# A decayed running sum behind a matrix product: another order of the channels on the partitions

## The chip, the cores and the metric

The kernel runs on one core of a Trainium2 chip. The core has five engines that work side by side, each through its own list of instructions in order: TensorE (PE in the profile; its weight loads are PEld) multiplies matrices, VectorE (DVE), ScalarE (ACT) and GpSimd (POOL) work on elements, SyncE (SP) issues transfers. Transfers (DMAs) move data between the main memory and the on-chip memory SBUF, which has 128 partitions; TensorE writes its products to a second on-chip memory, PSUM. Engines wait for each other and for transfers through semaphores.

The metric is the device time of one execution in microseconds (us). The profile shows one such execution, in which each instruction has a start and a duration.

## The reference

```python
def setup_inputs():
    B, S, D = (16, 2048, 1024)
    return {'x': np.random.randn(B, S, D).astype(np.float32), 'w': np.random.randn(D, D).astype(np.float32), 'decay': (0.9 * np.random.rand(D) + 0.05).astype(np.float32)}

def reference(x, w, decay):
    xw = x @ w
    out = np.zeros_like(xw)
    out[:, 0, :] = xw[:, 0, :].copy()
    for t in range(1, S):
        out[:, t, :] = decay[None, :] * out[:, t - 1, :] + xw[:, t, :]
    return out.astype(np.float32)
```

A product of 32768 rows with a 1024 x 1024 matrix, and then, along each of 16 sequences of 2048 steps, a running sum per output channel in which the sum so far is multiplied by that channel's decay at each step.

## The kernel before, in words

**Tiling.** The rows are cut into 64 chunks of 512 time steps (`TL`), and two chunks form a group, except that the last two are taken one by one. Each group (or single chunk at the end) gives eight output tiles `n` of 128 output channels: 31 x 8 + 2 x 8 = 264 tiles. A tile is the product of eight weight blocks `k` (`K` = 8), accumulated in PSUM, 512 columns per matmul.

**How x gets onto the partitions.** The product needs the 1024 input channels on the partitions. `load` (line 105, issued on GpSimd's queue, four transfers per chunk) brings a chunk into `xb` and converts it to bfloat16 on the way: partition 32q + t' holds, for each of 16 blocks of 32 time steps (`j`), the 256 channels of quadrant q at time step t' of the block. These 256 channels are 128 words of 4 bytes, each a pair of neighbouring channels. `turn` (line 115) then has VectorE transpose blocks of 32 partitions x 32 words into `xw`, so that time runs along the row and each partition holds four words' worth (`M` = 4) of channels. The instruction takes an access pattern for its input: per block j and per m, 32 words `c` that go to the 32 partitions of the quadrant. `part` (line 123, ScalarE mostly) splits the pairs, from `xw` into `xt`, the operand of the matmuls. There are 62 turns of a whole chunk (2048 words per partition) and, for the first two chunks, 16 turns of an eighth each (256 words), so that work can start early.

**How w gets there.** `w` must lie with the same input channels on the same partitions. It comes in four quarters `(h, e)`: h is the half of the output columns (512 of them), e the even or odd channel of the pairs. `load_w` (line 313) loads a quarter into a staging area (`stage`) by four transfers. The first quarter goes over the queues of SyncE and ScalarE (two each), the other three over GpSimd's, between and behind the transfers of the first chunks of x. `settle` (line 320) copies one m of a quarter, 128 partitions x 512 columns, into the weights `wsb` as bfloat16; VectorE and ScalarE share these copies. The opening's order of work is written out in `agenda[-99]`: M are half chunks of x, U the later quarters of w, W and w the settles (VectorE and ScalarE), E the turns of an eighth, F and G the parts.

**From the tile to the output.** A tile's running sum is formed in one of two ways. Unpaired: VectorE scans the PSUM tile directly (`run`, line 233, 1024 elements). Paired: ScalarE copies the tile to `xs` (line 186) and multiplies its even steps by the decay (line 169), GpSimd adds them to the odd steps (`join`, line 208), VectorE scans the 512 sums with the squared decay (line 213), ScalarE multiplies the results by the decay (`even`, line 169) and GpSimd fills in the other steps (`fill`, line 260). Paired operations read or write every second element of a row, a step of 8 bytes. At the end VectorE transposes the tile back (`back`, line 272), and when four tiles of a group are there, SyncE's queue stores them (line 296).

**Order.** All instructions are pinned in program order per engine. `agenda` writes the order out for the first 34 tiles and the last 20; between them `usual` does, per tile, the copy of this tile, the scan and the completion of the last one, the output turn of the one before, and `later` puts the turns (T) and parts (X, Y) of a coming chunk at fixed tiles ahead of their use: two full turns per group of eight tiles. VectorE thus has, in one list, the turns, the scans and the output turns.

Of the kernel before, what the change touches and what calls it, by code (L numbers as in the profile page):

```python
# [14 lines left out]
def _ap(ap_obj: bass.AP, new_ap, extra_offset=0):  # L15
    return dataclasses.replace(
        ap_obj,
        ap=[list(p) for p in new_ap],
        offset=ap_obj.offset + extra_offset,
    )  # L20
# [5 lines left out]
def kernel(  # L26
# [27 lines left out]
    pin = tc.keep_in_program_order  # L54
    B, S, D = x.shape
# [3 lines left out]
    P = 32  # L59
    CQ = D // NQ  # L60
    K = CQ // P
    M = K // 2
# [4 lines left out]
    CH = D // 2  # L67
# [8 lines left out]
    def ring(pool, name, count, shape, dtype=FP32):  # L76
        i = turns[name] = turns.get(name, -1) + 1
        return pool.tile(shape, dtype, name=f"{name}{i % count}")

    def quad(q):  # L80
        return slice(q * P, (q + 1) * P)
# [28 lines left out]
    def turn(c, j0=0, j1=NJ, m0=0, m1=M):  # L110
        if c not in xw_of:
            xw_of[c] = ring(sb, "xw", 2, [128, M, NJ, P, 2], BF16)
        src = xb_of[c][:, j0:j1].rearrange("p j c -> p (j c)").bitcast(FP32)
        dst = xw_of[c].rearrange("p m j i e -> p (m j i e)").bitcast(FP32)
        pin(nc.vector.transpose(  # L115
            out=dst.rearrange("p (m j i) -> p j m i", m=M, i=P)[:, j0:j1, m0:m1],
            in_=src.rearrange("p (j m c) -> p j m c", m=M, c=P)[:, :, m0:m1]))

    def part(c, copy, m0, m1, j0=0, j1=NJ):
        if c not in xt_of:  # L120
# [159 lines left out]
    class Outlet:  # L280
# [8 lines left out]
        def store(self, b, t0):  # L289
# [4 lines left out]
            for j in range(0, self.nj, nj):  # L294
# [11 lines left out]
    stage = {(0, 0): room[0][:, 0:size],  # L306
             (0, 1): room[0][:, size:size * 3 // 2].bitcast(BF16),
             (1, 0): room[1][:, 0:size // 2].bitcast(BF16),
             (1, 1): room[1][:, size // 2:size].bitcast(BF16)}

    def load_w(queues, h, e):
        for i, q in enumerate((0, 2, 1, 3)):
            pin(queues[i % len(queues)].dma_start(  # L313
                out=stage[h, e][quad(q)].rearrange("p (m d) -> p m d", m=M),
                in_=_ap(w, [[2 * D, P], [2 * P * D, M], [1, CH]],
                        (q * CQ + e) * D + h * CH)))

    def settle(h, e, m, copy):
        src = stage[h, e][:, m * CH:(m + 1) * CH]
# [5 lines left out]
    rows = const.tile([128, 2, P], FP32, name="rows")  # L325
    touch = const.tile([128, 1], BF16, name="touch")
    load_w((nc.sync, nc.scalar), 0, 0)
    pin(nc.vector.memset(idle, 0.0))  # L328
    pin(nc.vector.memset(rows, 0.0))
# [13 lines left out]
    for q in range(NQ):  # L343
        pin(nc.sync.dma_start(
            out=rows[q * P:q * P + R],
            in_=_ap(decay, [[P, R], [CH, 2], [1, P]], q * CR)))
# [10 lines left out]
    def load_part(i):  # L357
        load_w((nc.gpsimd,), *((0, 1), (1, 0), (1, 1))[i])
# [76 lines left out]
    def turn_and_load(c):  # L435
        turn(c)
        if 2 <= c < nch - 3:
            loads.extend((c + 3, q) for q in range(NQ))
# [14 lines left out]
        "M": load_half,  # L453
        "U": load_part,
        "E": lambda i: turn(i // 8, *halves[i // 4 % 2], i % 4, i % 4 + 1),
        "F": lambda i: part_one(i, nc.vector.tensor_copy),
        "G": lambda i: part_one(i, nc.scalar.copy),
# [218 lines left out]
```

## Time and profile before

| | |
|---|---|
| time, median of 3 runs | 904.32 us (903.89 to 904.64) |
| profiled execution, time | 904.34 us |
| profiled execution, span of the core | 902.5 us |
| mean granted TensorE clock | 0.999 of full speed |
| busy: TensorE / VectorE / ScalarE / GpSimd | 896.7 / 824.2 / 686.9 / 656.6 us |
| full turns, line 115 | 62 x 2284 ns |
| turns of an eighth, line 115 | 16 x 414 ns |
| issues of w on GpSimd, line 313 | 12 x 544 ns |

The span runs from the first to the last instruction that the profile shows; what is missing to the execution's time, 904.34 - 902.5 = 1.84 us, lies around it. In lines on groups of instructions, the columns are line, engine, operation, output <- input, shapes, count, then busy us, mean ns of one instruction, and after the second bar the idle time of the engine just before them with what ended it. In a timeline each line has start, duration, engine, line and operation, with the idle time before it in brackets. In lines on waits, the numbers are us in total, how many times, and the longest.

### The profile page before, as it was taken

Reading aid. Unit: us, or ns where it says so; the run is one execution under the profiler, and the core shown is the slowest. Engines: PE = TensorE matmul, PEld = TensorE weight load, DVE = VectorE, ACT = ScalarE, POOL = GpSimd, SP = SyncE. Lnnn points to the kernel's source line nnn. Section 1 sums busy time; section 2 is a strip of 40 time slices with the busy share of each in tenths; the row PEclk is TensorE's granted clock in tenths of the full one; section 3 lists DMA queues with packets and bytes.
Section 4 is the critical chain, followed back from the end, with each engine's and each line's share of the span. In section 5 each row is a group of like instructions: output and inputs, shape, how many; then the busy total and the mean of one; then the engine's idle time right before and its main releaser. Section 6 shows DMA issues by size and latency. Waiting matters only on the chain.

```text
span 902.5 us, 12285 instructions
## 1 busy us (share of the span) xinstructions
PE 896.7 (99%) x4201; PEld 411.4 (46%) x4201; DVE 824.2 (91%) x632; ACT 686.9 (76%) x958; POOL 656.6 (73%) x755
## 2 busy tenths in 40 slices
PE   9999999999999999999999999999999999999998
PEld 5544444444444444444444444444444444444444
DVE  4999998998999999999998999999999999999998
ACT  4889867777877877878778778777787787787743
POOL 7888678777767768777677687777777776876632
PEclk9999999999999999999999999999999999999999
DMA  9999999999999999999999999999999999999858
GB/s 193 194 215 220 231 231 206 215 231 243 251 249 248 242 251 246 244 250 253 227 236 228 221 228 230 232 227 227 232 230 228 227 234 223 228 226 218 183 142 236
DMA packets 403182, 204.77 MB, mean 227 GB/s; under 512 B 9392, under 2 KB 402096, under 8 KB 403120
## 3 DMA queue, kind: packets, MB, share of 16 engines
q1 hardware_dynamic: 265808, 134.77, 60.8%
q0 software_dynamic: 137024, 68.70, 56.8%
q8 instruction: 33, 0.54, 0.2%
q10 hardware_dynamic: 288, 0.52, 0.2%
q14 instruction: 29, 0.24, 0.1%
HBM read 138.42 MB, written 134.22 MB: 302 GB/s over the span
## 4 chain that ended last, share of the span: by engine, by line
PE 98%; DMA 1%; POOL 0%; issue 0%; DVE 0%; DVEq 0%; POOLq 0%
PE ps L131 96%; PE spare L131 1%; DMA xb<-in_x_dram 1%; DMA ot<-in_w_dram 1%; POOL ot L313 0%; PE spare L398 0%; PE ps L398 0%; DVE h L416 0%; DVE wsb L320 0%; DVEq L320 0%; POOLq L660 0%
## 5 line engine op out<-in xcount | busy, mean ns | idle before, releaser
L131 PE MATMUL ps<-xt,wsb 128*128 128x512 bf16 x4016 | 866.1, 378 | 0.5 <-DVE wsb L320 0.5
L131 PEld LDWEIGHTS <-wsb 128*128 128x128 bf16 x4152 | 405.9, 98 | 479.7 <-ACT wsb L320 0.8
L208 POOL TENSOR_TENSOR xs<-h,xs 128x512 f32<-128x512 f32 (+1 forms) x190 | 242.5, 1276 | 187.1 <-ACT h L169 85.5
L186 ACT COPY xs<-ps 128x1024 f32<-128x1024 f32 (+1 forms) x190 | 188.9, 994 | 152.8 <-PE ps L131 147.7
L272 DVE STREAM_TRANSPOSE ot<-so 128x1024 f32<-128x1024 f32 (+2 forms) x264 | 300.1, 1175 | 4.5 <-DMA out_dram<-ot 2.3
L260 POOL TENSOR_TENSOR so<-h,xs 128x512 f32<-128x512 f32 (+1 forms) x190 | 241.1, 1271 | 45.2 <-ACT h L169 28.0
L123 ACT COPY xt<-xw 128x2048 bf16<-128x2048 bf16 (+1 forms) x136 | 242.2, 1789 | 7.8 <-DVE xw L115 7.8
L105 POOL DMA_DIRECT2D xb<-in_x_dram x264 | 174.0, 660 | 3.5 <-DMA ot<-in_w_dram 1.1
L169 ACT ACTIVATE h<-so,dec 128x512 f32<-128x512 f32 (+1 forms) x190 | 145.4, 766 | 29.8 <-DVE so L213 26.7
L115 DVE STREAM_TRANSPOSE xw<-xb 128x2048 f32<-128x2048 f32 (+1 forms) x78 | 147.3, 1900 | 7.0 <-DMA xb<-in_x_dram 7.0
L213 DVE TENSOR_TENSOR_SCAN so<-spare,keep,xs 128x512 f32<-128x512 f32 (+1 forms) x97 | 119.8, 1237 | 25.7 <-POOL xs L208 25.4
L213 DVE TENSOR_TENSOR_SCAN so<-spare,xs 128x512 f32<-128x512 f32 x93 | 113.1, 1218 | 26.5 <-POOL xs L208 23.6
L169 ACT ACTIVATE h<-ps,dec 128x512 f32<-128x512 f32 (+1 forms) x189 | 129.4, 685 | 0.0
L233 DVE TENSOR_TENSOR_SCAN so<-dec,ps 128x1024 f32<-128x1024 f32 x34 | 76.7, 2259 | 1.0 <-ACT h L169 1.0
L233 DVE TENSOR_TENSOR_SCAN so<-dec,keep,ps 128x1024 f32<-128x1024 f32 (+2 forms) x35 | 75.4, 2153 | 0.0
L264 ACT COPY keep<-so 128x1 f32<-128x1 f32 x136 | 25.2, 188 | 9.4 <-DVE so L233 9.0
L204 ACT COPY so<-keep 128x1 f32<-128x1 f32 x97 | 18.5, 192 | 2.7 <-DVE ot L272 2.5
L131 PE MATMUL spare<-xt,wsb 128*128 128x512 bf16 (+1 forms) x56 | 11.9, 341 | 0.0
L131 PE MATMUL ps<-xw,wsb 128*128 128x256 bf16 (+1 forms) x68 | 11.2, 301 | 0.0
L202 POOL MEMSET so<- 128x1 f32 x93 | 10.6, 116 | 0.6 <-DVE ot L272 0.6
L313 POOL DMA_DIRECT2D ot<-in_w_dram x12 | 6.5, 544 | 3.2 <-DMA xb<-in_x_dram 2.1
L338 PE MATMUL spare<-idle 128*128 128x512 bf16 x22 | 7.5, 519 | 1.2 <-DVE idle L328 1.2
(39 smaller groups left out, 39.3 us busy)
## 6 DMA issues: line engine op xcount, KB each, us to landing
out_dram<-ot SPq DMA_DIRECT2D x236, 512.0 KB, 10.9
xb<-in_x_dram POOLq DMA_DIRECT2D x248, 256.0 KB, 7.9
out_dram<-ot SPq DMA_DIRECT2D x56, 128.0 KB, 2.6
xb<-in_x_dram POOLq DMA_DIRECT2D x16, 128.0 KB, 5.8
out_dram<-ot SPq DMA_DIRECT2D x8, 256.0 KB, 4.2
ot<-in_w_dram POOLq DMA_DIRECT2D x12, 128.0 KB, 5.1
out_dram<-xb SPq DMA_DIRECT2D x3, 256.0 KB
ot<-in_w_dram ACTq DMA_DIRECT2D x2, 256.0 KB, 5.1
```

The lines of the kernel that those rows point to most:

```text
L105: pin(nc.gpsimd.dma_start(out=xb_of[c][quad(q), j0:j1], in_=_ap(x, [[D, P], [P * D, j1 - j0], [1, CQ]], (b * S + t0 + j0 * P) * D + q * CQ)))
L115: pin(nc.vector.transpose(out=dst.rearrange("p (m j i) -> p j m i", m=M, i=P)[:, j0:j1, m0:m1], in_=src.rearrange("p (j m c) -> p j m c", ...
L123: pin(copy(out=xt_of[c][:, m0:m1, :, j0 * P:j1 * P], in_=src))
L131: pin(nc.tensor.matmul(out=ps[:, t0:t1] if ps.shape[1] >= t1 else ps, lhsT=lhs, rhs=rhs, start=(k == 0 and t0 == start), stop=(k == K - 1),))
L169: pin(nc.scalar.activation(out=h, in_=src, func=mybir.ActivationFunctionType.Copy, scale=dec[:, self.n:self.n + 1]))
L186: pin(nc.scalar.copy(out=self.xs[:, i * size:(i + 1) * size], in_=ps))
L208: pin(nc.gpsimd.tensor_tensor(out=odds, in0=self.g, in1=odds, op=ALU.add))
L213: pin(nc.vector.tensor_tensor_scan(out=so[:, 3:T + 2:2], data0=squares[-1][:, n:n + 1].to_broadcast([128, T // 2]), data1=self.xs[:, 1:T:2 ...
L233: pin(nc.vector.tensor_tensor_scan(out=so[:, t + 2:t + 2 + size], data0=dec[:, n:n + 1].to_broadcast([128, size]), data1=ps, initial=befor ...
L260: pin(nc.gpsimd.tensor_tensor(out=self.so[:, 2:T + 2:2], in0=self.h, in1=self.xs[:, 0:T:2], op=ALU.add))
L264: pin(nc.scalar.copy(out=self.keep, in_=self.so[:, self.T + 1:self.T + 2]))
L272: pin(nc.vector.transpose(out=outlet.ot[:, :, c0:c0 + P], in_=self.so[:, 2 + t0:2 + t0 + nj * P].rearrange("p (i t) -> p i t", t=P)))
```

## The change

Two access patterns change. In `before`, word 32m + c of a quadrant's 128 words goes to partition c of the quadrant, in block m: partition 32q + c holds channels 256q + 64m + 2c + e. In the changed kernel it is word 4c + m: partition p = 32q + c holds channels 8p + 2m + e, so that the 1024 channels lie at one stride of eight channels over all 128 partitions. The transposing instruction writes as before, and reads words that lie four words (16 bytes) apart within each run of 32, where it read neighbouring words.

The rows of w follow the same order. A quarter's four transfers were one per quadrant, each into 32 partitions with four rows of 512 columns per partition, from rows that lie two rows apart. Now there is one per m, each into all 128 partitions with one row of 512 columns per partition, from rows that lie eight rows apart. Bytes, transfers and their queues stay; a settle reads what one transfer brings, where it read parts of all four. Every engine issues the same instructions in the same order. Below line 317, line numbers are one lower in the changed kernel.

```diff
@@ turn
         pin(nc.vector.transpose(
             out=dst.rearrange("p (m j i) -> p j m i", m=M, i=P)[:, j0:j1, m0:m1],
-            in_=src.rearrange("p (j m c) -> p j m c", m=M, c=P)[:, :, m0:m1]))
+            in_=src.rearrange("p (j c m) -> p j m c", m=M, c=P)[:, :, m0:m1]))
@@ load_w
     def load_w(queues, h, e):
-        for i, q in enumerate((0, 2, 1, 3)):
-            pin(queues[i % len(queues)].dma_start(
-                out=stage[h, e][quad(q)].rearrange("p (m d) -> p m d", m=M),
-                in_=_ap(w, [[2 * D, P], [2 * P * D, M], [1, CH]],
-                        (q * CQ + e) * D + h * CH)))
+        for m in range(M):
+            pin(queues[m % len(queues)].dma_start(
+                out=stage[h, e][:, m * CH:(m + 1) * CH],
+                in_=_ap(w, [[K * D, 128], [1, CH]], (2 * m + e) * D + h * CH)))
```

## The prediction

> **What bounds the kernel now.** I read the totals first, then the chain that ended last, then the windows by stage, then VectorE's groups, waits and timeline. The totals and the chain, from the page:
>
> ```profile
> PE 896.7 (99%) x4201; PEld 411.4 (46%) x4201; DVE 824.2 (91%) x632; ACT 686.9 (76%) x958; POOL 656.6 (73%) x755
> ...
> PE 98%; DMA 1%; POOL 0%; issue 0%; DVE 0%; DVEq 0%; POOLq 0%
> ```
>
> TensorE is the bound: busy for 896.7 of 902.5 us, and 98% of the chain. VectorE (DVE) comes next, with 902.5 - 824.2 = 78.3 us idle in the whole span. Where that idle lies, by windows (columns: PE, weight loads, DVE, ACT, POOL, clock, DMA share, GB/s):
>
> ```profile
> 0.00:28.00 28.00, 26.35 (x155) 15.54 (x156) 13.42 (x40) 14.94 (x28) 21.79 (x42) 1.00 1.22 194
> 28.00:56.00 28.00, 28.00 (x130) 12.46 (x129) 27.89 (x22) 25.54 (x40) 24.67 (x31) 1.00 1.43 202
> 56.00:84.00 28.00, 28.00 (x132) 12.73 (x130) 28.00 (x20) 25.22 (x29) 23.20 (x28) 1.00 1.30 216
> ...
> 392.00:504.00 112.00, 112.00 (x521) 50.77 (x520) 103.58 (x74) 87.50 (x119) 82.82 (x93) 1.00 1.21 236
> ...
> 840.00:868.00 28.00, 28.00 (x131) 12.71 (x130) 25.14 (x18) 18.02 (x24) 13.87 (x16) 1.00 0.69 164
> 868.00:902.50 34.50, 30.39 (x156) 15.23 (x154) 30.44 (x40) 13.99 (x41) 10.58 (x16) 0.97 0.76 206
> ```
>
> From 28 to 84 us DVE has nothing to spare, and in the steady state it is busy for 103.58 of 112 us, with PE full throughout. Idle is 14.6 us in the first 28, 2.9 + 4.1 = 7.0 in the last 62.5, and 78.3 - 21.6 = 56.7 between. The groups on DVE (shapes apart), then its waits between 60 and 840 us, then a stretch of its timeline:
>
> ```profile
> L272 DVE STREAM_TRANSPOSE ot<-so 128x1024 f32<-128x1024 f32 x248 | 292.3, 1215 | 4.4 <-DMA out_dram<-ot 2.3 <-POOL so L202 1.1 <-POOL so L260 0.4
> L115 DVE STREAM_TRANSPOSE xw<-xb 128x2048 f32<-128x2048 f32 x62 | 141.6, 2284 | 2.0 <-DMA xb<-in_x_dram 2.0
> L233 DVE TENSOR_TENSOR_SCAN so<-dec,ps 128x1024 f32<-128x1024 f32 x34 | 76.7, 2259 | 1.0 <-ACT h L169 1.0
> L115 DVE STREAM_TRANSPOSE xw<-xb 128x256 f32<-128x256 f32 x16 | 5.7, 414 | 5.0 <-DMA xb<-in_x_dram 5.0
> L233 DVE TENSOR_TENSOR_SCAN so<-dec,spare 128x512 f32<-128x512 f32 x1 | 1.2, 1189 | 0.0
> ```
>
> ```profile
> DVE so L213 <- POOL xs L208: 47.2, 61, 1.3
> ```
>
> ```profile
> 503.71 2.29 DVE L115 STREAM_TRANSPOSE xw<-xb 128x2048 f32<-128x2048 f32 x1
> 505.95 1.28 DVE L213 TENSOR_TENSOR_SCAN so<-spare,keep,xs 128x512 f32<-128x512 f32 x1
> 507.20 1.25 DVE L272 STREAM_TRANSPOSE ot<-so 128x1024 f32<-128x1024 f32 x1
> 509.40 1.28 DVE L213 TENSOR_TENSOR_SCAN so<-spare,keep,xs 128x512 f32<-128x512 f32 x1 [0.96 <-POOL xs L208]
> ```
>
> Of the 56.7 us between, 47.2 are waits of a scan for GpSimd's join, and 5.8 are one wait each for two DMAs and two GpSimd results. These are slack: if DVE is late, they shrink. The other 3.7 have no wait named, and stay. Idle that stays whatever DVE does is thus 14.6 + 7.0 + 3.7 = 25.3 us. The slack, 78.3 - 25.3 = 53.0 us, comes a microsecond at a time behind each turn.
>
> **The turns.** Every full turn reads 2048 4-byte words per partition, side by side today; afterwards words that follow each other in reading order lie four words (16 bytes) apart. Writing is unchanged, and so are counts and order on every engine: 62 full turns and 16 eighths (256 words), 62 + 16/8 = 64 full turns' worth. The price of a dense word is (2284 - 414) / 1792 = 1.04 ns. What a word costs at 16 bytes is not in this trace. The widest step that any engine takes here between single words is 8 bytes (the paired scan, ScalarE's and GpSimd's odd and even passes).
>
> Low end: nothing added, as the dense row has it. High end: the slowest words in the trace that are read and written with a step, GpSimd's join, 1276 ns for 512, 2.49 ns a word; a turn would gain 2048 x (2.49 - 1.04) = 2.97 us. Between them lies DVE's own scan at (2259 - 1189) / 512 = 2.09 ns a word, two of the dense turn's steps. I take that value: my assumption is that a word fetched without its neighbour costs a second step, and this is the trace's row for DVE at that pace, on DVE's own port. A full turn becomes 2284 + 2048 x (2.09 - 1.04) = 4.43 us, 2.15 more; an eighth gains 0.27. DVE's added work is 62 x 2.15 + 16 x 0.27 = 137.6 us.
>
> The paired scan gives no way out: it steps by 8 bytes in 1189 to 1277 ns per 512 words, like the scan of dense words, but at 2.09 ns a word it would hide such a cost.
>
> [...]
>
> **Where this lies.** 137.6 us against 53.0 of slack: DVE becomes the bound. New span = 824.2 busy + 25.3 idle that stays + 137.6 = 987.1 us; outside the span lie 904.34 - 902.5 = 1.84, so 988.9 us. The profiled execution (904.34) stands 0.02 above the median, so nothing is corrected. Breakeven is 53.0 / 64 = 0.83 us per turn, 0.40 ns per word.
>
> Behind a longer turn on DVE wait, in program order, a scan (whose result ScalarE's even pass and GpSimd's fill want), an output turn (whose stores go out on SP's queue) and, off DVE, ScalarE's copies of xw into xt. All are late with DVE. TensorE then stops for lack of a free PSUM tile: an unpaired tile is freed by DVE's scan, a paired one by ScalarE's copy, which stands behind the even pass. ACT (76%) and POOL (73%) gain no work and get slack, so the wait for the join should disappear.
>
> In the opening, four eighths take 2.7 instead of 1.4 us; this is already in the 137.6.
>
> **The loads of w.** The issues stay: 2 on SP, 2 on ACT, 12 on POOL; each still moves 128 rows of 2 KB. A POOL issue is 542 ns; the nearest dearer row is an issue for x at 660, so at most 12 x 0.12 = 1.4 us on POOL, spread over 8 to 24 us. I take 0; the work that hides it is POOL's waiting for landed DMAs (2.1 and 1.1 us). Each settle now waits for one transfer of a quarter, not four. Landing is 4.7 to 5.1 us for these transfers now; the trace has 2.6 (small stores) to 15.8 (x, behind others). What can be won are the waits before it, by the timeline of the opening:
>
> ```profile
> 14.93 0.69 DVE L320 COPY wsb<-ot 128x512 bf16<-128x512 bf16 x3 [0.85 <-DMA ot<-in_w_dram]
> 15.28 0.82 PE L131 MATMUL ps<-xt,wsb 128*128 128x512 bf16 x3 [0.46 <-DVE wsb L320]
> 24.09 1.04 DVE L320 COPY wsb<-ot 128x512 bf16<-128x512 bf16 x4 [2.01 <-DMA ot<-in_w_dram]
> ```
>
> That is at most 0.85 + 2.01 = 2.9 of DVE's kept idle, or 0.46 of TensorE's. What can be lost: DVE waits longer by whatever w lands later, up to 10.7 us by the worst row. I take 0: bytes, rows and the queue are the same, and x is in the same queue ahead of it.
>
> [...]
>
> **Rivals.**
>
> 1. The stride is free, and the kernel isn't slower. DVE at 91% never binds; TensorE's chain decides. For it: the dense row alone, and ScalarE's even pass, which reads at 8 bytes in 766 ns where a dense ScalarE cast of 512 words takes 616. Against: that pass already pays something, and 16 bytes is twice the step. Place: line 115; it holds up to 0.83 us per turn. Time: 904.3, less at most PE's 0.46 us: 903.9 to 904.3. To be faster by more than 0.2% (1.8 us; about what a measurement of this kernel can tell from no change) x too would have to land earlier, since TensorE's first product (10.93) waits for it. Chance 0.11.
> 2. A half price: every second word pays a second step, 0.52 ns on average, 1.07 us per turn. 64 x 1.07 = 68.5, so 824.2 + 25.3 + 68.5 + 1.84 = 919.8. Chance 0.21 for the stretch from there to halfway to my forecast (about 955), and 0.03 for less. For it: a step that changes every other fetch only. [...]
> 3. The dear end: 2.97 us per turn, 64 x 2.97 = 190; 1041 us. For it: it is the pace of an engine that reads with a step; against: GpSimd's pace is for another engine with two inputs. Chance 0.21 for 1015 to 1045. [...]
> 4. DVE bound, but waits don't vanish, since a turn of 4.4 us makes the pipeline lumpy: up to half of the 47.2 us stays, 1012. It is part of the forecast's upper stretch.
>
> **How the numbers follow.** Forecast (two steps a word, 955 to 1015): 0.42; the others as given; beyond 1045: 0.02. The time is 989. The range leaves out rival 1, what is beyond 1045 and the cheapest part of rival 2, and holds 0.42 + 0.21 + 0.21 = 0.84: 920 to 1045. Faster by over 0.2%: 0.03; within 0.2%: 0.08 (both from rival 1); slower by over 0.2%: 0.89.
>
> **What would show it.** The full turn's row: 4.4 us (2.28 is rival 1, 3.4 rival 2, 5.3 rival 3). DVE's busy time near 962 us, 97% of the span; PE's still near 897, 91%; the chain mostly DVE; the wait for the join under 10 us; ACT's waits for PE turned into waits for DVE. The other DVE groups (1215, 2259) unchanged. I am wrong if the turn's row is under 3.1 us, or if it is longer and the span follows 849.5 + 64 x (added per turn) by more than 15 us off, which would mean that slack and bound are misread; or if w lands so late that DVE's idle in the first 28 us grows past 20.

## The result: 2.9% slower

The changed kernel takes 930.41 us (median of 6 runs, 930.27 to 931.15) against 904.35 us before (6 runs, 903.89 to 904.82): 1.029 times as long, 95% interval 1.0276 to 1.0303. That is 26.1 us more, where 84.6 were forecast. Its profiled execution has a span of 928.6 us.

The totals and the chain, from the page of the changed kernel:

```profile
PE 907.5 (98%) x4201; PEld 411.5 (44%) x4201; DVE 909.3 (98%) x632; ACT 677.4 (73%) x958; POOL 659.2 (71%) x755
...
DVE 48%; issue 34%; DMA 9%; SPq 2%; POOL 2%; PE 1%; ACT 1%; DVEq 1%; POOLq 0%; ACTq 0%
```

The bound has moved: VectorE's share of the span went from 91 to 98%, and TensorE's share of the chain from 98 to 1%. By stage (windows, columns as before):

```profile
56.00:84.00 28.00, 24.43 (x112) 10.83 (x111) 28.00 (x19) 21.98 (x26) 16.85 (x19) 1.00 1.23 220
...
112.00:140.00 28.00, 27.32 (x119) 11.93 (x119) 28.00 (x20) 20.31 (x30) 14.05 (x11) 0.94 0.78 168
...
392.00:504.00 112.00, 111.43 (x514) 50.08 (x513) 112.00 (x74) 84.53 (x117) 82.60 (x93) 1.00 1.16 226
```

VectorE has no idle left in these stages. The 19.3 us that it is idle in the whole span lie almost all in the first 28 us (11.3), between 140 and 168 us (3.7) and behind 868 us (4.0). From 112 to 140 us the granted TensorE clock is 0.94, where it was 1.00 before; VectorE is busy through all of that window, so the clock does not explain the loss there. The weight loads, one per matmul, tell how far TensorE got. In the steady state 520 of them fit into 112 us before, 0.215 us each. Between 28 and 168 us there are 588 where there were 650, so 62 x 0.215 = 13.3 us are lost in that stretch; before 28 us 4 of them, 0.9 us; in the six windows of 112 us from 168 to 840 together 41, 8.8 us; the remaining 3 us lie behind. More than half of the loss is thus made in the first 168 us. Of the missing loads 44, or 9.5 us, fall between 28 and 112 us. There VectorE had nothing to spare: the prediction shows it busy for 27.89 and 28.00 of 28 us in the kernel before, and the next window of that kernel reads:

```profile
84.00:112.00 28.00, 28.00 (x132) 12.64 (x131) 27.92 (x21) 25.54 (x36) 19.71 (x22) 1.00 1.28 229
```

The groups on VectorE, shapes apart:

```profile
L272 DVE STREAM_TRANSPOSE ot<-so 128x1024 f32<-128x1024 f32 x248 | 317.0, 1422 | 1.8 <-POOL so L202 1.4 <-POOL so L260 0.4
L115 DVE STREAM_TRANSPOSE xw<-xb 128x2048 f32<-128x2048 f32 x62 | 256.9, 4143 | 0.0
L213 DVE TENSOR_TENSOR_SCAN so<-spare,keep,xs 128x512 f32<-128x512 f32 x90 | 130.9, 1457 | 0.0
L115 DVE STREAM_TRANSPOSE xw<-xb 128x256 f32<-128x256 f32 x16 | 8.8, 610 | 5.7 <-DMA xb<-in_x_dram 5.7
```

The full turn went from 2284 to 4143 ns, the eighth from 414 to 610. The scans and the output turns seem to have become slower too (1277 to 1457, 1215 to 1422 ns). They have not, as a stretch of the timeline shows:

```profile
511.60 4.18 DVE L115 STREAM_TRANSPOSE xw<-xb 128x2048 f32<-128x2048 f32 x1
515.50 1.45 DVE L213 TENSOR_TENSOR_SCAN so<-spare,keep,xs 128x512 f32<-128x512 f32 x1
516.66 1.42 DVE L272 STREAM_TRANSPOSE ot<-so 128x1024 f32<-128x1024 f32 x1
517.80 1.44 DVE L213 TENSOR_TENSOR_SCAN so<-spare,keep,xs 128x512 f32<-128x512 f32 x1
518.96 2.52 DVE L233 TENSOR_TENSOR_SCAN so<-dec,keep,ps 128x1024 f32<-128x1024 f32 x1
```

Each instruction begins some 0.28 us before the record of the one ahead ends. What counts for the engine is the distance from one start to the next: 515.50 - 511.60 = 3.90 us for this turn, 1.16 and 1.14 for the scan and the output turn behind it, which is less than before (1.25 and 1.24 in the stretch shown there, idle time left out). Over the whole trace, worked out from all starts, a full turn takes 3.856 us to the next start where it took 2.282: 1.574 us more.

The waits of VectorE and of ScalarE's even pass:

```profile
ACT h L169 <- DVE so L213: 198.0, 116, 4.2
...
DVE so L213 <- POOL xs L208: 1.9, 2, 1.3
```

The scan's wait for the join, 49.0 us in the whole span before, has gone; ScalarE waits 198 us for VectorE's scans.

### The profile page after: what moved, and what is told of

Its sections match the earlier page's. It is cut to its first block, busy times and chain, and to the rows that moved or that the text cites. A ratio compares the mean times of both kernels' runs of the same rounds, so it can differ in the third digit from the quotient of the medians.

```text
span 928.6 us, 12274 instructions
## 1 busy us (share of the span) xinstructions
PE 907.5 (98%) x4201; PEld 411.5 (44%) x4201; DVE 909.3 (98%) x632; ACT 677.4 (73%) x958; POOL 659.2 (71%) x755
## 4 chain that ended last, share of the span: by engine, by line
DVE 48%; issue 34%; DMA 9%; SPq 2%; POOL 2%; PE 1%; ACT 1%; DVEq 1%; POOLq 0%; ACTq 0%
DVE so L213 24%; DVE ot L272 16%; DMA out_dram<-ot 6%; DVE xw L115 5%; DMA xb<-in_x_dram 3%; DVE so L233 3%; SPq L296 2%; PE ps L131 1%; POOL xb L105 1%; ACT h L169 1%; DVEq L272 1%; POOL so L260 0%; POOL xs L208 0%; ACT xt L123 0%; DVEq L115 0%
## 5 line engine op out<-in xcount | busy, mean ns | idle before, releaser
L131 PE MATMUL ps<-xt,wsb 128*128 128x512 bf16 x4016 | 875.9, 379 | 14.8 <-DVE so L233 10.1
L260 POOL TENSOR_TENSOR so<-h,xs 128x512 f32<-128x512 f32 (+1 forms) x190 | 242.3, 1277 | 168.2 <-ACT h L169 110.1
L272 DVE STREAM_TRANSPOSE ot<-so 128x1024 f32<-128x1024 f32 (+2 forms) x264 | 325.2, 1374 | 1.8 <-POOL so L202 1.4
L115 DVE STREAM_TRANSPOSE xw<-xb 128x2048 f32<-128x2048 f32 (+1 forms) x78 | 265.7, 3419 | 5.7 <-DMA xb<-in_x_dram 5.7
L213 DVE TENSOR_TENSOR_SCAN so<-spare,keep,xs 128x512 f32<-128x512 f32 (+1 forms) x97 | 136.8, 1418 | 0.0
L213 DVE TENSOR_TENSOR_SCAN so<-spare,xs 128x512 f32<-128x512 f32 x93 | 129.7, 1396 | 2.0 <-POOL xs L208 1.9
L233 DVE TENSOR_TENSOR_SCAN so<-dec,ps 128x1024 f32<-128x1024 f32 x34 | 83.7, 2476 | 0.3 <-PE ps L131 0.3
L233 DVE TENSOR_TENSOR_SCAN so<-dec,keep,ps 128x1024 f32<-128x1024 f32 (+2 forms) x35 | 81.8, 2336 | 0.0
L204 ACT COPY so<-keep 128x1 f32<-128x1 f32 x97 | 18.5, 192 | 4.7 <-DVE ot L272 4.5
```

What stands on the lines that cost most here:

```text
L115: pin(nc.vector.transpose(out=dst.rearrange("p (m j i) -> p j m i", m=M, i=P)[:, j0:j1, m0:m1], in_=src.rearrange("p (j c m) -> p j m c", ...
L131: pin(nc.tensor.matmul(out=ps[:, t0:t1] if ps.shape[1] >= t1 else ps, lhsT=lhs, rhs=rhs, start=(k == 0 and t0 == start), stop=(k == K - 1),))
L213: pin(nc.vector.tensor_tensor_scan(out=so[:, 3:T + 2:2], data0=squares[-1][:, n:n + 1].to_broadcast([128, T // 2]), data1=self.xs[:, 1:T:2 ...
L233: pin(nc.vector.tensor_tensor_scan(out=so[:, t + 2:t + 2 + size], data0=dec[:, n:n + 1].to_broadcast([128, size]), data1=ps, initial=befor ...
L260: pin(nc.gpsimd.tensor_tensor(out=self.so[:, 2:T + 2:2], in0=self.h, in1=self.xs[:, 0:T:2], op=ALU.add))
L272: pin(nc.vector.transpose(out=outlet.ot[:, :, c0:c0 + P], in_=self.so[:, 2 + t0:2 + t0 + nj * P].rearrange("p (i t) -> p i t", t=P)))
```

## The experiments

In the following, "added" is what a full turn takes from its start to the next start, beyond the 2.28 us of the kernel before, as a mean over all 62 full turns of the trace; where part of a turn is done twice, both are counted. Where a run changes only the opening, the windows tell.

**The stepped read alone, and w by quadrant.** The old transfers, with rows eight apart so that they fit the new order:

```diff
-            in_=src.rearrange("p (j m c) -> p j m c", m=M, c=P)[:, :, m0:m1]))
+            in_=src.rearrange("p (j c m) -> p j m c", m=M, c=P)[:, :, m0:m1]))
...
-                in_=_ap(w, [[2 * D, P], [2 * P * D, M], [1, CH]],
+                in_=_ap(w, [[K * D, P], [2 * D, M], [1, CH]],
```

> One part alone: turns read with the 16-byte step, w comes by quadrant in four transfers as before (its rows eight apart within a quadrant, so that they match). Theory A, the stepped read is the whole loss: 930 us give or take 1, full turns at 4.1 us, DVE at 98%, as with the whole change. Rival B, the new transfers of w take part of the 26 us: under 925 us. Rival C, the new transfers give something back in the opening: above 931 us.

932.32 us (931.09 to 932.88, 4 runs) beside 904.13 before: 1.0307 (1.029 to 1.0324), with 1.57 us added per turn, as in the changed kernel. The loss does not need the new transfers: it is 28.2 us here, 2.1 above that of the whole change, which by the expectation's numbers is rival C. In its profile the first settles on VectorE start later than before or in the changed kernel:

```profile
9.21 0.76 DVE L320 CAST wsb<-ot 128x512 bf16<-128x512 f32 x2 [7.70 <-DMA ot<-in_w_dram]
```

They started at 7.30 before and at 4.59 in the changed kernel. The first 28 us hold 140 weight loads where the changed kernel has 152, which is 12 x 0.215 = 2.6 us, so the difference lies in the opening. It cannot be read as a gain of the new transfers, since this form of w is not that of the kernel before either; why w lands late in it stays open.

**The new form of w, with dense turns.** One transfer per m, from the rows of the old order:

```diff
...
+                in_=_ap(w, [[CQ * D, NQ], [2 * D, P], [1, CH]], (2 * P * m + e) * D + h * CH)))
```

> The other part alone: turns read neighbouring words as before; w comes with one transfer per m into all 128 partitions, from the rows that the old order of channels needs. Theory A: within 1 us of 904.3, full turns at 2.28 us. Rival B: above 908 us. Rival C: under 903 us. In the opening, the first settles should start at about 4.5 us in place of 7.3, and x should land some 0.5 us later than 9.7 if it is the transfers of w that push it back in the changed kernel.

918.68 us (917.05 to 919.62), 1.0157 (1.0142 to 1.0172): above 908, but not for rival B's reason. The turns are dense (2285 ns), the steady state is that of before (520 weight loads in 112 us), and everything is lost in the opening:

```profile
0.00:28.00 28.00, 15.99 (x67) 7.67 (x69) 6.24 (x24) 7.32 (x15) 13.21 (x26) 0.82 0.78 118
```

In 28 us, 69 weight loads where the kernel before has 156, at 118 GB/s instead of 194. The first quarter's four settles start at 8.49, 13.33, 16.43 and 18.70 us. The pattern of these transfers differs from the changed kernel's in its outermost dimension, 4 instead of 128. The trace shows what is slow: the 512 packets of 2 KB of the first quarter take 0.11 us each, as before, but on average 3.5 of them are under way at once instead of 12.1, and they last from 2.19 to 18.30 us instead of from 1.77 to 6.34. Whether that dimension is the cause was not shown, since no run here varied it alone. As a test of the change's own form of w the run fails; the one with pairs, below, stands in for it.

**Half the step.** Words two apart (8 bytes):

```diff
...
+            in_=src.rearrange("p (j g c f) -> p j g f c", g=2, c=P, f=2)
...
+                in_=_ap(w, [[CQ * D, NQ], [4 * D, P], [1, CH]],
```

> The step of the read is halved: words lie two words (8 bytes) apart, with the rows of w to match, one transfer per m. Theory P, a word is dear as soon as its neighbour in memory is not the next one read: the same as at 16 bytes, full turns at 4.1 us, 930 us. Rival L, what counts is that two reads in a row fall into the same 16 bytes: 8 bytes is free, full turns at 2.28 us, 904 us. Something between, 3.2 us and some 912 us, if the cost grows with the step.

```profile
L115 DVE STREAM_TRANSPOSE xw<-xb 128x2048 f32<-128x2048 f32 x62 | 141.8, 2287 | 0.7 <-DMA xb<-in_x_dram 0.6
```

The turn is as fast as the dense one, 2287 against 2284 ns, as theory L has it and P does not. The time, 917.41 us (1.0145, 1.013 to 1.016), is that of the run before it, which has the same form of w and the same slow opening; it says nothing of the turns. At this step no word is followed by its neighbour, so a word is not dear for that alone.

**Pairs of neighbouring words, a hop of 32 bytes between pairs,** with w by one transfer per m over 128 partitions:

```diff
+            out=dst.rearrange("p (m a b) -> p m a b", m=M, b=2)[:, m0:m1, j0 * P // 2:j1 * P // 2],
+            in_=src.rearrange("p (a m b) -> p m a b", m=M, b=2)[:, m0:m1]))
...
+                in_=_ap(w, [[2 * K * D, 64], [2 * D, 2], [1, CH]], (4 * m + e) * D + h * CH)))
```

> The read goes in pairs of neighbouring words with a hop of 32 bytes from pair to pair; the rows of w to match, one transfer per m over all 128 partitions. Theories P and L both: pairs are free, full turns at 2.28 us, 904 us within 1. Rival: any hop costs, at half the price since every second word hops: full turns at 3.1 us, 908 to 915 us.

```profile
L115 DVE STREAM_TRANSPOSE xw<-xb 128x2048 f32<-128x2048 f32 x62 | 141.8, 2286 | 2.8 <-DMA xb<-in_x_dram 2.7
```

904.40 us (904.24 to 904.91, 10 runs) beside 904.13: 1.0003 (0.9994 to 1.0012). Pairs with this hop are free: 2286 against 2284 ns. And w by row sets over all 128 partitions, here with 64 as its outermost dimension, is worth nothing: the first settles start at 4.23 us in place of 7.26, but x lands later, so that the first turn of an eighth starts at 10.37 instead of 9.72 us. TensorE's first product needs that turn's result as well as the settles', so the earlier settles win nothing: that product starts at 11.02 us, and at 10.93 before. Nor do the earlier settles show that w as a whole lands sooner: a settle now needs one transfer, where before it needed parts of all four. The last settle of the quarter, which waits for the last of the four transfers, starts at 7.87 us in this run and at 6.42 in the changed kernel; before, all four had landed by 7.26. So w as a whole does not land sooner in both.

**The same amount of dense work.** To test the slack without any stepped read: the kernel before, with a part of each full turn done a second time.

```diff
     def turn_and_load(c):
         turn(c)
+        turn(c, 0, 8)      # then 12, then 16 of the 16 blocks
```

> The kernel before, with the first 8 of 16 blocks of every full turn done a second time (1024 neighbouring words, same data to the same place): about 1.1 us more of VectorE behind each full turn, and no stepped read. By the prediction's slack (0.83 us per turn): 851.3 + 62 x 1.1 = 920 us. By what the stages of the changed kernel show (no slack for the turns of the opening, about 1.4 us per turn afterwards): the opening loses some 9 us, the steady state nothing: 913 us.

> The same with 12 of 16 blocks: about 1.65 us more per full turn, what a stepped turn costs from start to next start. Theory A, the stepped read acts only as VectorE time: within 2 us of the changed kernel's 930.4. Rival D, stepped reads also slow the other engines at the memory or the opening: clearly under 928 us, the difference being what they take elsewhere. By the prediction's slack it would be 954 us.

> The same with all 16 blocks, a whole second turn: about 2.2 us more per turn, the price that the prediction took. If only its price was wrong: 989 us. If its slack was wrong as well: 904 + 20 in the opening + 40 in the steady state, 964 us.

| run | added per turn, us | time, us | before beside it | more, us | 62 x added - more |
|---|---|---|---|---|---|
| 8 blocks again | 1.203 | 913.85 (913.62 to 914.11) | 903.99 | 9.9 | 64.7 |
| the changed kernel | 1.574 | 930.41 | 904.35 | 26.1 | 71.5 |
| 12 blocks again | 1.732 | 939.10 (939.01 to 939.33) | 903.99 | 35.1 | 72.3 |
| 16 blocks again | 2.267 | 972.34 (972.27 to 972.41) | 903.99 | 68.4 | 72.2 |

The ratios are 1.0109 (1.0094 to 1.0124), 1.0389 (1.0372 to 1.0406) and 1.0756 (1.074 to 1.0772). With 8 blocks the time is the 913 us read from the stages, not the 920 of the prediction's slack. With 12 blocks the run came out above the 930.4 that theory A gave, because it added 1.73 us a turn, where the expectation had 1.65 and the stepped read adds 1.57. With 16 blocks it lies between the two values expected, 8 us above the nearer. Set against what each run really added, the last column is the answer: from 1.57 us up, dense or stepped, the time is that of before + 62 x added - 72 us. A stepped read therefore acts as VectorE time and, within 1 us, as nothing else, and the slack is 72 us, not 53. The run with 8 blocks lies where both regimes meet: 604 weight loads between 28 and 168 us instead of 650 are 46 x 0.215 = 9.9 us, its whole loss, and afterwards it keeps the pace of before (519 per 112 us).

Where the additional slack comes from shows in the run with 16 blocks (timeline):

```profile
506.10 4.62 DVE L115 STREAM_TRANSPOSE xw<-xb 128x2048 f32<-128x2048 f32 x2
510.64 1.19 DVE L213 TENSOR_TENSOR_SCAN so<-spare,xs 128x512 f32<-128x512 f32 x1
511.75 1.21 DVE L272 STREAM_TRANSPOSE ot<-so 128x1024 f32<-128x1024 f32 x1
512.88 1.19 DVE L213 TENSOR_TENSOR_SCAN so<-spare,xs 128x512 f32<-128x512 f32 x1
```

Scan to output turn 1.11 us, output turn to scan 1.13. Over the whole trace, with idle time left out, the scans of 512 elements (183 paired ones and 9 others) take 1.139 us each from start to start where they took 1.184 in the kernel before, the output turns of 1024 elements 1.133 instead of 1.168. Times 192 and 248 that is 8.6 + 8.7 = 17.3 us of busy time that is not there once VectorE is always behind; the turns stay as they were (2.257 us each, 2.258 before). Busy time says the same: 946.4 us in this run, where 824.2 + 62 x 2.267 = 964.8 would be expected, 18.4 less. Why instructions follow each other more closely when none has to wait stays open.

**Other steps.** Full turns only, on the kernel before; these read other words than the product needs, so the result is another one, and only durations and times are used.

```diff
+            in_=_ap(src, [list(src.ap[0])] + [[128, NJ], [1, M], [3, P]])   # words 3 apart
...
+            in_=_ap(src, [list(src.ap[0])] + [[64, NJ], [1, M], [8, P]])    # 8, 16, 24, 32 apart
```

> Full turns read words three apart (12 bytes); eighths and w as before. Which words are read is changed, so the output is another one; only the duration of the turn is asked. If a word is dear when it is alone in its 16 bytes: two words of four are, 2.24 + half of 1.6 = 3.0 us from start to next start. If every step above 8 bytes costs the same: 3.85 us. If a cost grows with the step in bytes: 3.0 to 3.4 us.

> Full turns read words eight apart (32 bytes), with other words read than the product needs. If the price is one new 16-byte piece per word: 3.85 us from start to next start, as at 16 bytes, and 930 us. If it grows with the step: above 4.2 us.

> Full turns read words 24 apart (96 bytes), with other words read than the product needs. One price for every step from 16 bytes on: 3.85 us from start to next start, 930 us. [...]

> Full turns read words 16 apart (64 bytes), with other words read than the product needs. Added per turn from start to next start, after 1.60 us at 32 bytes and 2.95 at 96: about 2.3 us, 972 us in all, if the price grows evenly with the step; 1.60 and 928 us if 96 bytes is a special case; 2.95 and 1012 us if there are two prices with the border between 32 and 64 bytes.

> Full turns read words 32 apart (128 bytes), with other words read than the product needs. About 3.6 us more per turn and some 1050 us if the price grows evenly with the step; 1.60 and 928 us if 96 bytes is a special case; 2.95 and 1012 us if there are two prices.

| step, bytes | turn to next start, us | added, us | time, us | 62 x added - more |
|---|---|---|---|---|
| 4 (before) | 2.28 | 0 | | |
| 8 | 2.29 | 0.01 | (slow opening) | |
| 12 | 2.95 | 0.670 | 908.74 | 36.8 |
| 16 (the change) | 3.86 | 1.574 | 930.41 | 71.5 |
| 32 | 3.83 | 1.546 | 927.98 | 71.9 |
| 64 | 3.62 | 1.339 | 915.63 | 71.3 |
| 96 | 5.19 | 2.903 | 1011.76 | 72.2 |
| 128 | 3.72 | 1.435 | 921.35 | 71.5 |

The times at 12 bytes and from 32 bytes on are single runs, set against 904.01 us (12, 32 and 96 bytes) and 903.93 us (64 and 128) beside them; the durations are means over 62 turns. At 12 bytes, where of each four words two share their 16 bytes, the price is less than half of that at 16, as the first of the expectations said. From 16 bytes on it stays within 1.34 to 1.57 us, except at 96 bytes:

```profile
L115 DVE STREAM_TRANSPOSE xw<-xb 128x2048 f32<-128x2048 f32 x62 | 327.0, 5274 | 0.3 <-DMA xb<-in_x_dram 0.3
```

None of the three expectations for 64 and 128 bytes came true exactly: the price doesn't grow with the step, there are not two prices with a border, and 96 bytes is a special case beside steps that are not quite equal. Why is open. At 96 bytes, 5.19 us to the next start, less the 0.15 us that a dense turn takes beyond its words (2.28 - 2048 x 0.00104), are 2.46 ns a word. At the change's own step the word costs 1.04 + 1574/2048 = 1.81 ns.

## Why the prediction was wrong in size

**Right.** The read with a step of 16 bytes is dear, VectorE becomes the bound, the wait for the join goes (1.9 us), ScalarE waits for VectorE, and w plays no part in the sum. The idle that stays was 25.3 us by forecast. It is 970.6 - 946.4 = 24.2 in the run with 16 blocks and 928.6 - 909.3 = 19.3 in the changed kernel, where the longer eighths take up 3.1 us of what was idle. The rival with a free stride, and with it every gain, is excluded by the turn's row.

**Wrong, first: the price of a word, the step "I take that value".** The scan's 2.09 ns a word was taken; measured are 1.81. With the eighths, 137.6 us were added; the full turns add 62 x 1.574 = 97.6. The eighths cost nothing that can be seen: the last column is 71.5 for the changed kernel, which has them stepped, and 71.3 to 72.3 for runs that have them dense, though they took 16 x 0.196 = 3.1 us longer. They lie in the first 28 us, where VectorE waits 5.7 us for x right ahead of them. Together that is 40.0 us of the miss. The scan was the wrong row because it takes 2.09 ns on words that lie side by side too, so its pace says nothing of a step; that it was exactly two dense steps made it look like a price for reads. That a word without its neighbour costs a second step was an assumption, and at 8 bytes, where no neighbour follows either, the turn takes 2287 ns; that the scan's pace is that of a port of VectorE is shown by no run. The measured time lies in the stretch given to rival 2, and that is in part luck: its 1.07 us per turn was too low and its slack too small, and the two errors offset each other. A dense load of 1.203 us per turn already took only 913.85 us, below the 919.8 that rival 2 gave for 1.07.

**Wrong, second: the slack, the step "Idle that stays".** The sum 824.2 + 25.3 treated VectorE's busy time as fixed work and only its idle time as slack, 53.0 us. But part of the busy time itself disappears when instructions stand in the queue: 17.3 us in the scans and output turns of the run with 16 blocks. In the changed kernel the sum closes: VectorE's idle fell from 78.3 to 19.3 us, by 59.0, of which the eighths took 3.1, and it was busy for 909.3 us where 824.2 + 97.6 + 3.1 = 924.9 would be expected, 15.6 less. 59.0 - 3.1 + 15.6 = 71.5 us of slack, 18.5 more than the 53.0. That is the other 19 us. The prediction named its own alarm for this, a span more than 15 us off 849.5 + 64 x added: that form gives 950.2 for 1.574 us, and the span is 928.6.

Both together: 904.35 + 97.6 - 72 = 929.95, measured 930.41. The forecast of 988.9 was off by 58.5 us, of which 40 are price and 19 are slack.

**Missed in the list of what would show it.** A turn's row of 4.4 us was expected and 4.14 found, which looks like a hit; from start to start it is 3.86. Busy time near 962 us was expected: 909.3. The chain was to be mostly VectorE: it is 48%, with 34% "issue", time in which the profile shows no wait. The other VectorE groups were to be unchanged: their rows rose by 0.2 us, without taking more of the engine's time. The prediction's "2.7 instead of 1.4 us" for four eighths sets the sum of four records against the time that four overlapping ones cover; covered, they take 2.2 us.

## What to carry to other kernels

The dense fp32 transpose of 2048 words on VectorE could be given a step of 8 bytes (2287 against 2284 ns), or pairs of words with a hop of 32 bytes (2286 ns; no other hop was tried), for nothing, but not single words 16 bytes apart: that cost 0.77 ns a word. Where an order of channels can be built from such pairs, that is the one to try first: here it cost nothing (904.40 us against 904.13). The slack of an engine was not its idle time (72 us against 53.0): measure it by adding known work in the place in question (here the same instruction once more), and read durations as distances between starts once an engine has a queue (a stepped turn has a record of 4.14 us and takes 3.86). VectorE, at 91% over the span, had almost no slack between 28 and 112 us (83.8 of 84 us busy), and more than a third of the loss came from there (9.5 of 26.1 us).

## What was not expected of the hardware

- The price of a stepped read is not a smooth function of the step: 1.57, 1.55, 1.34, 2.90 and 1.43 us per turn of 2048 words at 16, 32, 64, 96 and 128 bytes.
- With turns at a step of 16 bytes the records of VectorE's scans and output turns become about 0.2 us longer and overlap (output turn 1422 ns instead of 1215), without the engine doing less; the output turn's record is 1315 ns at 32 bytes, 1403 at 64 and 1471 at 128. At 12 bytes (1217 ns), at 96 (1224) and with each turn done twice (1208) it hardly grows.
- The scans of 512 elements follow each other in 1.139 instead of 1.184 us, and the output turns in 1.133 instead of 1.168, in the run with 16 blocks, where VectorE is always behind.
- With w by transfers over 128 partitions whose outermost dimension is 4, the opening was late (69 weight loads in the first 28 us instead of 156): 918.68 us in all against 904.13.
